# Fewer scheduling turns between k-tiles in two mixers of a three-block kernel

## The chip, the cores and the metric

The kernel runs on one core of a Trainium2 chip. The metric is the device time of one execution in microseconds (us); the kernel before took 1020.08 us, the median of three runs (1019.89 to 1020.59).

## The reference

Input is x, 256 positions by 1024, with a memory of 256 by 1024. Two blocks of a first model follow each other, then one block of a second. Every block is x = x + mixer(norm(x)) @ w_out and then x = x + ffn(norm(x)), all in float32, and norm is a root mean square norm with gains. Cut to what matters:

```
u = norm(x) @ w_in                      # 1024 x 2560 in blocks 0 and 1
block 0: o = silu(g) * norm(retention(q, k, v))           # 6 heads, chunk-causal
block 1: o = norm(softmax(q1 k1) - lam * softmax(q2 k2)) v  # 6 heads, causal by chunks
both:    o_mem = softmax(qc . mk) mv    # 4 heads over the normed memory
         x = x + concat(o, o_mem) @ w_out
         x = x + (silu(h @ w_gate) * (h @ w_up)) @ w_down  # inner width 2816
block 2: z, xbc, dt, q, k, v, f = split(norm(x) @ w_in_2)  # 1024 x 5664
         y1 = gated norm of a chunked state-space scan (16 heads) of conv(xbc), dt, z
         y2 = forgetting attention (16 heads) of q, k, v, with decays from f
         x = x + concat(y1, y2) @ w_out_2
         x = x + (silu(gate) * val) @ w_down_2             # gate, val after a causal conv
```

## The kernel before, in words

All of x stays on the chip as two tiles of 128 positions. A product with a weight runs as three matmuls in the fast fp32r type: operand and weight are each split into a high and a low part (names wh and wl for weights, lth and ltl for the normed, transposed activations), and high x high, high x low and low x high are summed in PSUM (mm3). A weight arrives by DMA in units of two k-tiles (UK = 2) by 512 columns into st; ScalarE casts it to wh, VectorE subtracts for wl. There are four st buffers and six of wh and of wl.

A projection (proj) makes 512 columns for both position tiles t: for each unit of two k-tiles and each t it issues two k-tiles of three matmuls, eight k-tiles per t, and behind the last k-tile of a t the evacuation from PSUM to SBUF.

Everything else is written as tasks: Python generators that issue some instructions (transposes, small matmuls, softmax steps, norms, splits) and then yield. A planner (class Weave) keeps a model clock per engine and runs at build time; the order in which it issues is the order of each engine's queue on the chip. A projection gives tasks a turn by W.poll(): it steps every task whose inputs are ready by the model more than 0.1 us ago (LAG), and ends with a call of W.fill(). fill issues the weight DMAs, casts and subtractions for which buffers are free. join runs tasks until a named one is done, and lets the model's TensorE stand still until then. A projection calls W.poll() behind each k-tile but the last of a t, and once behind each evacuation. The output projections (acc) call it behind each k-tile of six matmuls.

mixer0 runs seven projections: chunks 0, 1, 2, the memory's keys and values for block 0 (kv0), chunk 4, those for block 1 (kv1), chunk 3. Chunk 0 is run with a function `first` that issues the start of the program by hand. Beside them run the tasks of retention for three pairs of heads (qk, pair_task), of the memory's norm and keys, and of the memory attention (mem_attn). w_out then joins, per pair of k-tiles in the order 4, 6, 0, 2, the task that makes these: pair 2, the memory attention, pair 0, pair 1.

mixer2 runs twelve projections: two of 272 columns (bc_proj), then q, k, v, xbc and z for the first half of the heads, then the same five for the second. Beside them run gates, decays, fox (the attention), xs_part and ssd. Its w_out joins the first half's tasks and the second's in turns.

All engine calls go through one helper, so that the profile has the one line L89 for them; groups are told apart by the names of tiles: psm and psa are PSUM tiles, pcol is the identity for transposes.

Of the kernel before, what the change touches and what calls it, by code (L numbers as in the profile page):

```python
# [21 lines left out]
UK = 2  # L22
# [77 lines left out]
class Weave:  # L100
# [65 lines left out]
    def go(self, gen, at=None):  # L166
        t = Task(gen, self.now if at is None else at)
        self.tasks.append(t)
        return t
# [38 lines left out]
    def join(self, *ts):  # L208
        while not all(t.done for t in ts):
            t, at = self._next()  # L210
            assert t is not None and at < NEVER, "tasks wait for each other"
            self.clock["T"] = max(self.now, at)
            self._step(t, at)
            self.fill()
        return [t.val for t in ts]


def build(tc, a, out, stop=None):
    with tc.manual_schedule():
        _build(tc, a, out, stop)  # L220


def _build(tc, a, out, stop):
    nc = tc.nc
    W = Weave()
# [107 lines left out]
    def bcast(r, d):  # L333

        return r.unsqueeze(2).to_broadcast([r.shape[0], r.shape[1], d])

    def rep(ap, n):

        return ap.unsqueeze(1).to_broadcast([ap.shape[0], n, ap.shape[1]])
# [4 lines left out]
    def g128(ap):  # L344
        return ap.rearrange("p (g d) -> p g d", d=P)
# [15 lines left out]
    def unit_hi(parts=None, last=True):  # L361
        u, n = ready[prog["hi"]], plan[prog["hi"]][3]
        if u[1] is None:
            u[1] = whi.get(True)
        for k in parts or (slice(0, UK),):
            S.copy(u[1][:, k, :n], u[0][:, k, :n])
        prog["hi"] += last

    def unit_lo(parts=None, last=True):
        u, n = ready[prog["lo"]], plan[prog["lo"]][3]  # L370
        if u[2] is None:
            u[2] = wlo.get(True)
        for k in parts or (slice(0, UK),):
            V.tensor_tensor(u[2][:, k, :n], u[0][:, k, :n], u[1][:, k, :n].bitcast(F32), op=ALU.subtract)
        if last:
            stage.close(u[0])
        prog["lo"] += last

    AHEAD = 100

    def fill():

        while True:
            now, did = W.now, False
            if prog["dma"] < len(plan) and stage.free_at() < NEVER:
                unit_dma()
                did = True
            i = prog["lo"]
            if i < prog["hi"] and W.done[ready[i][1][:].tensor.name] <= now + AHEAD and wlo.free_at() <= now + AHEAD:
                if i <= prog["use"] + 1 or W.clock["V"] <= now + AHEAD:  # L390
                    unit_lo()
                    did = True
            i = prog["hi"]
            if i < prog["dma"] and W.done[ready[i][0][:].tensor.name] <= now + AHEAD and whi.free_at() <= now + AHEAD:
                if i <= prog["use"] + 1 or W.clock["S"] <= now + AHEAD:
                    unit_hi()
                    did = True
            if not did:
                return
# [3 lines left out]
    def unit(w, k0, c0, n, more=None):  # L403

        i = prog["use"]
        assert plan[i] == (w, k0, c0, n, more), (i, plan[i][1:], (k0, c0, n, more))
        while prog["lo"] <= i:
            if prog["dma"] <= i:
                unit_dma()
            if prog["hi"] <= i:  # L410
                unit_hi()
            else:
                unit_lo()
        prog["use"] += 1
        return ready.pop(i)[1:]

    def drop(u):
        whi.close(u[0])
        wlo.close(u[1])

    def mm3(ps, l, wh, wl, start, stop, late=False):
        T.matmul(ps, l[0], wh, start=start, stop=False)
        a, b = (l[0], wl), (l[1], wh)
        for i, (x, y) in enumerate((b, a) if late else (a, b)):
            T.matmul(ps, x, y, start=False, stop=stop and i == 1)

    def proj(w, H, c0, n, evac, serial=False, more=None, first=None):


        ps, units = [None, None], {}  # L430

        def run(t, k0):
            if first:
                first(t, k0)
            if k0 not in units:
                units[k0] = unit(w, k0, c0, n, more)
            hi, lo = units[k0]
            if ps[t] is None:
                ps[t] = psm.get(True)
            for k in range(UK):  # L440
                if first and k:
                    first(t, k0 + k)
                mm3(ps[t][:, :n], H[t].lhs(k0 + k), hi[:, k, :n], lo[:, k, :n], k0 + k == 0, k0 + k == NKT - 1, first and k0 + k)
                if k0 + k < NKT - 1 and (not first or k0 + k > 5):
                    W.poll()
            if t == 1:
                drop(units[k0])
            if k0 == NKT - UK:
                evac(t, ps[t], H[t].scale())
                psm.close(ps[t])  # L450
                W.poll()

        ks = range(0, NKT, UK)
        for t, k0 in [(t, k0) for t in range(2) for k0 in ks] if serial else [(t, k0) for k0 in ks for t in range(2)]:
            run(t, k0)

        return go(iter(()), max(W.clock["S"], W.clock["V"]))
# [549 lines left out]
    def mixer0(H, nxt, first):  # L1007
# [6 lines left out]
        sqm[0] = ring(mx, 256, "sqm", 2)  # L1014

        def chunk(c, ev, first=None):
            for t in range(2):
                u[c, t] = mx.tile([P, 512], F32, tag=f"u{c % 3 if c < 4 else c}{t}", name=W.name("u"))
            E[c] = proj(w, H, c * 512, 512, ev, first=first)
# [96 lines left out]
        for nr in mT:  # L1116
            nr.drop()
        need = {0: [pt[0]], 2: [pt[1]], 4: [pt[2]], 6: [ma]}
        join(kv1)
        return w_out(a["w_out"][0], OUT0, oT, need, H, scope, nxt), kv1  # L1120

# [183 lines left out]
    def mixer2(H, nxt):  # L1305
# [88 lines left out]
        def fox_v(f):  # L1394
            vv = [vvr.get(True) for _ in range(2)]
            return vv, proj(w, H, 4624 + 512 * f, 512, lambda t, ps, r: S.activation(vv[t][:], ps[:], AF.Copy, scale=r))
# [104 lines left out]
        def bc_proj():  # L1501

            us = uxr.get(True)

            def ev(t, ps, r):
                S.activation(us[:, t * 512 + 272 : (t + 1) * 512], ps[:, :240], AF.Copy, scale=r)
                V.scalar_tensor_tensor(two(X[:])[:, t], ps[:, 240:272], r, prow[:, R_DT : R_DT + 32],
                                       op0=ALU.mult, op1=ALU.add)

            proj(w, H, 2048, 272,  # L1510
                 lambda t, ps, r: S.activation(us[:, t * 512 : t * 512 + 272], ps[:, :272], AF.Copy, scale=r), True)
            return us, proj(w, H, 2320, 272, ev, more=(5648, 16))
# [39 lines left out]
        def decays(g):  # L1552

            yield [gt]
            res = []
            for c in range(2):
                for hq in range(2):
                    h0 = 8 * g + 4 * hq
                    tas = []
                    for part in (Rh, Rl):  # L1560
                        yield tar, 1
                        tas.append(tar.get(True))
                        V.tensor_tensor(g128(tas[-1][:]), rep(tri[:], 4),
                                        bcast(part[:, 32 * c + h0 : 32 * c + h0 + 4].bitcast(F32), P), op=ALU.mult)
                    yield psa, 1
                    ps = psa.get(True)
                    for i, ta in enumerate(tas):
                        T.matmul(ps[:], onesr[:], ta[:], start=i == 0, stop=i == 1)
                        tar.close(ta)
                    yield dcr, 1  # L1570
                    dc = dcr.get(True)
                    for e in range(4):
                        V.tensor_scalar(dc[:, e * P : (e + 1) * P], ps[:, e * P : (e + 1) * P],
                                        cs[:, 32 * c + h0 + e : 32 * c + h0 + e + 1], 0.0, op0=ALU.subtract, op1=ALU.min)
                    psa.close(ps)
                    yield
                    S.activation(dc[:], dc[:], AF.Exp)
                    res.append(dc)
            yield
            return res  # L1580
# [99 lines left out]
        def z_proj(g):  # L1680
            zs = [zsr.get(True) for _ in range(2)]
            return zs, proj(w, H, g * 512, 512, lambda t, ps, r: S.activation(zs[t][:], ps[:], AF.Silu, scale=r))

        ubc = bc_proj()
        gt = go(gates(ubc[1]))
        q, nq = fox_qk(0, 0)
        k, nk = fox_qk(0, 1)
# [7 lines left out]
        k, nk = fox_qk(1, 1)  # L1695
        vv, got = fox_v(1)
        f1 = go(fox(1, (q, k), [nq, nk], vv, got, PACE2))
        dcs = go(decays(1))
        xs = go(xs_part(1, *xbc_proj(1)))
        s1 = go(ssd(1, dcs, xs, *z_proj(1)))  # L1700
# [188 lines left out]
```

## Time and profile before

| | before |
|---|---|
| median of 3 runs | 1020.08 us |
| profiled execution | 1019.89 us |
| its span, first to last instruction | 1018.1 us |
| TensorE matmuls busy | 1008.9 us, 99% of the span |
| VectorE busy | 691.0 us, 68% |
| ScalarE busy | 611.6 us, 60% |
| GpSimd busy | 67.8 us, 7% |
| moved by DMA | 191.69 MB, mean 188 GB/s |

The span is what the trace covers; the time of an execution is a little longer. Matmuls are pipelined and their ends are modelled, so that the durations of neighbours overlap: the distance between two starts tells what an instruction costs TensorE, not its duration. A non-transpose matmul in plain float32 shows as two instructions.

### The profile page before, as it was taken

What the parts mean: (1) busy time and instruction counts of PE and PEld (TensorE: products, weight loads), DVE (VectorE), ACT (ScalarE), POOL (GpSimd) and SP (SyncE); (2) the same over time, 40 slices, a digit from 0 to 9 for tenths busy, and PEclk for the clock granted to TensorE, in tenths of its full rate; (3) what the DMA queues carried; (4) which work ended last, traced back from release to release, by engine and by line L of the source; (5) the groups of instructions that cost most, each with busy time, mean ns of one, the idle gap of its engine ahead of it and who ended that gap; (6) DMA issues with size and microseconds to landing.
All of it is one profiled execution on the core that took longest, in us unless ns stands there. A gap on an engine that the chain in (4) does not pass through costs nothing.

```text
span 1018.1 us, 13938 instructions
## 1 busy us (share of the span) xinstructions
PE 1008.9 (99%) x5049; PEld 842.0 (83%) x5049; DVE 691.0 (68%) x1045; ACT 611.6 (60%) x982; POOL 67.8 (7%) x93
## 2 busy tenths in 40 slices
PE   8999999999999999999999999999999999999998
PEld 6888888888898778888888988888888888788887
DVE  5676566555556877756565467978788567878765
ACT  7557464444455887644444446686777557757753
POOL 1121000000001231100000001100300010000000
PEclk9999999999999999999999999999999999999999
DMA  7763567776564434577667457615621658887733
GB/s 248 260 221 125 165 189 225 243 229 190 185 220 160 145 121 128 170 246 248 185 227 236 153 149 216 202 42 165 186 84 66 203 161 281 261 273 223 258 125 114
DMA packets 120581, 191.69 MB, mean 188 GB/s; under 512 B 8256, under 2 KB 39744, under 8 KB 120384
## 3 DMA queue, kind: packets, MB, share of 16 engines
q1 hardware_dynamic: 120512, 190.80, 59.0%
q8 instruction: 40, 0.66, 0.3%
q14 instruction: 29, 0.24, 0.1%
HBM read 181.34 MB, written 9.44 MB: 187 GB/s over the span
## 4 chain that ended last, share of the span: by engine, by line
PE 93%; DVE 2%; ACT 2%; POOL 1%; DMA 1%; issue 1%; SPq 0%; ACTq 0%
PE psm L89 61%; PE psa L89 32%; POOL s8r L89 1%; DVE wl L89 0%; ACT pd L89 0%; DMA st<-w_in 0%; DMA fl<-scr 0%; DVE ltl L89 0%; ACT wh L89 0%; POOL s16r L89 0%; DVE s L89 0%; ACT lth L89 0%; DVE pd L89 0%; ACT qkT L89 0%; POOL s4r L89 0%
## 5 line engine op out<-in xcount | busy, mean ns | idle before, releaser
L89 DVE TENSOR_TENSOR wl<-st,wh 128x1024 fp32r<-128x1024 f32 (+2 forms) x339 | 388.0, 1168 | 189.6 <-ACT wh L89 185.9
L89 ACT CAST wh<-st 128x1024 fp32r<-128x1024 f32 (+2 forms) x339 | 334.1, 1007 | 217.8 <-PE psm L89 86.3
L89 PE MATMUL psm<-wh,lth 128*128 128x512 f32 (+2 forms) x1024 | 394.0, 385 | 1.0 <-ACT lth L89 1.0
L89 PE MATMUL psm<-wl,lth 128*128 128x512 f32 (+2 forms) x1024 | 385.6, 377 | 0.2 <-DVE wl L89 0.2
L89 PE MATMUL psm<-wh,ltl 128*128 128x512 f32 (+2 forms) x1024 | 381.0, 377 | 0.3 <-DVE ltl L89 0.2
L89 PEld LDWEIGHTS psm<-wh,ltl 128*128 128x128 f32 x1024 | 192.6, 188 | 36.6 <-DVE ltl L89 0.8
L89 PEld LDWEIGHTS psm<-wh,lth 128*128 128x128 f32 x1024 | 192.8, 188 | 34.8 <-ACT lth L89 1.4
L89 PEld LDWEIGHTS psm<-wl,lth 128*128 128x128 f32 x1024 | 192.9, 188 | 33.8 <-DVE wl L89 1.4
L89 PE MATMUL psa<-wh,lth 128*128 128x512 f32 x328 | 130.4, 398 | 0.0
L89 PE MATMUL psa<-wl,lth 128*128 128x512 f32 x328 | 128.0, 390 | 0.7 <-DVE wl L89 0.7
L89 PE MATMUL psa<-wh,ltl 128*128 128x512 f32 x328 | 105.1, 390 | 0.0
L89 PEld LDWEIGHTS psa<-wh,ltl 128*128 128x128 f32 x328 | 61.6, 188 | 13.1
L89 PEld LDWEIGHTS psa<-wl,lth 128*128 128x128 f32 x328 | 61.7, 188 | 12.9 <-DVE wl L89 1.1
L89 PEld LDWEIGHTS psa<-wh,lth 128*128 128x128 f32 x328 | 61.6, 188 | 11.8
L89 POOL TENSOR_SCALAR s1n<-s1n 128x1 f32<-128x1 f32 x14 | 5.4, 384 | 462.6 <-ACT sq L89 462.5
L89 DVE SCALAR_TENSOR_TENSOR cc<-na,ccol,cc 128x255 f32<-128x255 f32 (+1 forms) x64 | 27.2, 480 | 6.1 <-ACT cc L89 6.0
L89 DVE SCALAR_TENSOR_TENSOR sg<-psm,s1n,sg 128x512 f32<-128x512 f32 (+1 forms) x24 | 17.0, 706 | 19.8 <-PE psm L89 19.6
L89 ACT ACTIVATE sq<-xt 128x512 f32<-128x512 f32 x24 | 15.3, 636 | 22.9 <-DVE xt L89 22.2
L89 ACT ACTIVATE sg<-psm,s1n 128x512 f32<-128x512 f32 (+1 forms) x24 | 15.7, 653 | 18.7 <-PE psm L89 18.7
L89 ACT ACTIVATE uu<-psm,s1n 128x512 f32<-128x512 f32 (+1 forms) x24 | 15.6, 651 | 15.7 <-PE psm L89 15.6
L89 ACT ACT_TABLE_LOAD x16 | 20.5, 1283 | 5.0 <-PE psm L89 2.8
L89 POOL TENSOR_TENSOR s16r<-s16r,mhalf 128x16 f32<-128x16 f32 x7 | 22.2, 3178 | 0.6
(217 smaller groups left out, 856.4 us busy)
## 6 DMA issues: line engine op xcount, KB each, us to landing
st<-w_gate_up SPq DMA_DIRECT2D x80, 512.0 KB, 4.6
st<-w_in SPq DMA_DIRECT2D x67, 512.0 KB, 4.3
st<-w_down SPq DMA_DIRECT2D x66, 512.0 KB, 5.2
st<-w_up SPq DMA_DIRECT2D x40, 512.0 KB, 4.7
st<-w_out SPq DMA_DIRECT2D x32, 512.0 KB, 3.7
scr<-sq SPq DMA_DIRECT2D x64, 128.0 KB, 4.5
fl<-scr SPq DMA_DIRECT2D x16, 512.0 KB, 5.1
st<-w_in SPq DMA_DIRECT2D x30, 256.0 KB, 4.0
```

The lines of the kernel that those rows point to most:

```text
L89: f(*args, **kw)
```

## The change

A flag rare is set at every chunk of mixer0 and taken back behind the last one, and set in mixer2 ahead of bc_proj and taken back behind the second v projection. While it is set, proj calls W.poll() only behind the second k-tile of a unit and W.fill() behind the first. Chunk 0 keeps its turns, as do the turns behind evacuations, the output projections, mixer1, the feed-forward blocks and the last two projections of mixer2.

```diff
     AHEAD = 100
+    rare = [False]
...
                 if k0 + k < NKT - 1 and (not first or k0 + k > 5):
-                    W.poll()
+                    W.poll() if k == UK - 1 or first or not rare[0] else W.fill()
...
         def chunk(c, ev, first=None):
+            rare[0] = True
             for t in range(2):
...
         need = {0: [pt[0]], 2: [pt[1]], 4: [pt[2]], 6: [ma]}
+        rare[0] = False
         join(kv1)
...
+        rare[0] = True
         ubc = bc_proj()
...
         f1 = go(fox(1, (q, k), [nq, nk], vv, got, PACE2))
+        rare[0] = False
         dcs = go(decays(1))
```

## Rows read from the trace of the kernel before

**Rows 1.** The page: TensorE's busy time, and shares of the last chain by engine.

```profile
PE 1008.9 (99%) x5049; PEld 842.0 (83%) x5049; DVE 691.0 (68%) x1045; ACT 611.6 (60%) x982; POOL 67.8 (7%) x93
...
PE 93%; DVE 2%; ACT 2%; POOL 1%; DMA 1%; issue 1%; SPq 0%; ACTq 0%
```

**Rows 2.** Windows: stretch, length, busy (count) per engine, TensorE's clock, DMA share, GB/s.

```profile
20.80:107.50 86.70, 86.18 (x462) 71.25 (x462) 56.69 (x79) 57.48 (x96) 14.39 (x18) 1.00 0.61 201
...
618.00:736.00 118.00, 118.00 (x624) 99.64 (x623) 99.94 (x201) 87.41 (x157) 15.61 (x18) 1.00 0.52 157
...
40.29:43.29 3.00, 3.00 (x29) 3.00 (x28) 1.36 (x3) 1.44 (x4) 0.17 (x1) 1.00 1.06 388
```

**Rows 3.** Waits of TensorE, the longest: total us, times, longest us.

```profile
PE psa L89 <- DVE ones L89: 1.3, 1, 1.3
```

**Rows 4.** Timeline of TensorE, plain projection: start us, us, instruction, count.

```profile
64.19 0.39 PE L89 MATMUL psm<-wh,lth 128*128 128x512 f32 x1
...
68.72 0.39 PE L89 MATMUL psm<-wh,ltl 128*128 128x512 f32 x1
```

**Rows 5.** Timeline of TensorE: a run of four transposes, one of eight.

```profile
83.78 0.60 PE L89 MATMUL psa<-pcol,u 128*128 128x128 f32 x4
...
84.45 0.40 PE L89 MATMUL psm<-wl,lth 128*128 128x512 f32 x1
...
22.20 1.03 PE L89 MATMUL psa<-pcol,u 128*128 128x128 f32 x8
...
23.31 0.39 PE L89 MATMUL psm<-wl,lth 128*128 128x512 f32 x1
```

**Rows 6.** Timeline of TensorE: a run of eight 64-row matmuls, one of sixteen.

```profile
37.24 0.92 PE L89 MATMUL psa<-qkT 64*128 64x256 f32 x8
...
38.43 0.40 PE L89 MATMUL psm<-wl,lth 128*128 128x512 f32 x1
...
49.60 1.58 PE L89 MATMUL psa<-qkT 64*128 64x256 f32 x16
...
51.45 0.39 PE L89 MATMUL psm<-wl,lth 128*128 128x512 f32 x1
```

**Rows 7.** Timeline of TensorE: three projection matmuls between two runs.

```profile
55.23 0.48 PE L89 MATMUL psm<-wh,lth 128*128 128x512 f32 x1
...
56.01 1.50 PE L89 MATMUL psa<-u,sT 128*128 128x128 f32 x12
```

**Rows 8.** Timeline of TensorE and VectorE: the memory attention and its first use.

```profile
86.36 1.13 PE L89 MATMUL psa<-kT,mqT 64*128 64x256 f32 x8
...
88.32 1.13 PE L89 MATMUL psa<-kT,mqT 64*128 64x256 f32 x8
...
104.99 0.60 PE L89 MATMUL psa<-pcol,mo 128*128 128x128 f32 x4
...
107.52 0.69 DVE L89 TENSOR_TENSOR ltl<-psa,lth 128x512 fp32r<-128x512 f32 x1 [1.52 <-ACT lth L89]
...
113.84 0.39 PE L89 MATMUL psm<-wh,lth 128*128 128x512 f32 x1
```

**Rows 9.** Timeline of TensorE: the wait for the memory's keys.

```profile
70.08 0.39 PE L89 MATMUL psm<-wh,ltl 128*128 128x512 f32 x1
70.89 0.94 PE L89 MATMUL psa<-pcol,mk 128*128 128x128 f32 x4 [0.42 <-DVE mk L89]
```

**Rows 10.** Timeline of ScalarE: two weight casts with task work between them.

```profile
85.11 1.05 ACT L89 CAST wh<-st 128x1024 fp32r<-128x1024 f32 x1
...
94.31 1.09 ACT L89 CAST wh<-st 128x1024 fp32r<-128x1024 f32 x1
```

**Rows 11.** Timeline of TensorE: end of the first half's tasks, start of the output projection.

```profile
721.47 0.60 PE L89 MATMUL psa<-pcol,xd 128*128 128x128 f32 x4
...
780.08 0.48 PE L89 MATMUL psm<-wh,lth 128*128 128x512 f32 x1
```

## The prediction

> **What bounds the kernel now.** I read the page first: TensorE is busy 99% of the span, and the chain that ended last runs 93% on it, nearly all in the matmuls into psm and psa [rows 1]. The table by stretches then shows the two stretches that the change touches. [...] So TensorE's instruction order is the time. The change removes no matmul, no transpose, no copy and no transfer. It can gain only what lies between instructions on TensorE: what a change from projection to task work and back costs, and the few waits. It can lose only where a task that comes later is waited for.
>
> **What a turn is worth: the changes of work on TensorE.** Sixteen projections are touched (six in mixer 0 after the first, ten in the last mixer). Each has 16 turns now, 14 between k-tiles and 2 behind the evacuations, and 8 after, 6 and 2: 256 turns become 128. A k-tile is three matmuls. In a plain stretch 20 matmul starts take 68.72 - 64.19 = 4.53 us, 0.2265 us each [rows 4], so a k-tile is 0.68 us. The price of a change is read from starts: the time from the first task instruction to the second matmul after the run, less one matmul. Four transposes take 84.45 - 83.78 - 0.2265 = 0.4435 us and eight take 23.31 - 22.20 - 0.2265 = 0.8835 [rows 5]. The second four cost 0.440, so a run of transposes has a fixed part of 0.0035 us: leaving the projection for it is all but free. Runs on 64 rows differ: eight qkT matmuls take 38.43 - 37.24 - 0.2265 = 0.9635 us, sixteen take 51.45 - 49.60 - 0.2265 = 1.6235 [rows 6], so eight more cost 0.66 and the fixed part is 0.30 us.
>
> How many runs merge? In TensorE's timeline I count 18 runs of task work in the first stretch and 28 in the second. With a turn at every second k-tile, two runs can no longer be only three matmuls apart, and that is the case 13 times, 3 in mixer 0 and 10 in the last mixer; [rows 7] show the first. Each of those pairs merges or moves apart. I let all 13 merge. In one of the 13 both runs are 64-row work, the two blocks of the memory attention at 86.36 and 88.32 [rows 8]; I price it at 0.30 and the other twelve, nearest to transposes, at 0.0035: 0.30 + 0.04 = 0.34 us gained. The bounds are 0 (none merges, all move apart) and 13 x 0.30 = 3.9 us (every run costs what a 64-row run costs). I stay near the low end because 42 of the 46 runs are on 66 or 128 rows.
>
> **The wait that stands in the first stretch.** TensorE waits for the keys of the memory: 70.89 - 70.08 - 0.2265 = 0.58 us [rows 9]. Later turns can remove it, if the transposes move one k-tile on, or leave it, if they stand at a turn that stays. A chain of VectorE and GpSimd work sets it, not the turn, so I leave it in: 0, with bounds of -0.58 and +0.68 (the transposes go out at the same turn and the chain starts one k-tile later).
>
> **Weight splits.** The loading and splitting of weights keeps its call at every k-tile; what changes is that task work reaches ScalarE and VectorE in larger lots, ahead of a split in the same queue. The trace has such a lot: ScalarE casts a weight at 85.11 and the next at 94.31 [rows 10], 8.15 us without one, filled with the exponentials, and TensorE went on. The six weight buffers hold 6 x 12 matmuls, 16.3 us of projection. A lot that grows by one k-tile's work is still hidden: 0. Without the cover a split that comes late costs its own length, about 1 us. No DMA moves: the SyncE queue gets the same loads at the same calls, and the changed stretches issue nothing else. GpSimd's short chains (the norms' powers) start with their tasks and are waited for only by these.
>
> **Where tasks are waited for.** In the last mixer the work of the first half ends with the transposes at 721.47, and the output projection that needs it starts at 780.08 [rows 11]: 58 us of room, and the second half's attention mostly runs where each k-tile still has its turn. Cost 0. In mixer 0 the room is small. The memory attention's last transposes start at 104.99, ScalarE and VectorE split them by 107.52 + 0.69 = 108.21, and the output projection's second pair of k-tiles needs them from 113.84 on [rows 8]: 5.63 us. From the transposes of its queries at 83.78 [rows 5] to 104.99 its chain makes eight steps from one TensorE turn to the next. If each loses one k-tile the chain is 8 x 0.68 = 5.4 us later: covered, with 0.2 us left. I take 0, because steps that already lie two or four k-tiles apart need not lose any; a loss at all sixteen turns of the chain (each step has a copy or an exponential with a turn of its own) is 10.9 us, 5.3 us past the cover, and that is the other bound. Behind the late transposes nothing else on TensorE could go ahead: the wait stands in its queue, and everything after it shifts by the same amount.
>
> **Sum.** The profiled execution took 1019.89 us, 1.79 around its span of 1018.1. Less 0.34 this is 1019.55. The median of the three runs shown is 0.19 above that execution, so the forecast for the median is 1019.7 us.
>
> **Rivals.** (a) The memory attention comes late, on the slower side. For it speaks that its room is within 0.2 us of what eight lost turns use, and that a later turn also lets a weight cast of 1.05 us into ScalarE's queue ahead of the chain's next copy; against it, that half of the steps need lose nothing, and that the output projection gives turns of the full number again. Late by 1 to 2 us (ten or eleven lost turns) the time is 1020.7 to 1021.7; from twelve on (12 x 0.68 = 8.2 us, 2.5 past the cover) it is 1022.2 and counts as slower; at sixteen, 1025.0. (b) A change of work costs more than transposes show, as with the 64-row runs: at 0.15 for each of 13 and with the 0.58 us wait gone the gain is 2.5 us, 1017.6. For it speaks [rows 6], against it [rows 5]. (c) The change thins turns that hardly bind: tasks are ready later than the turn anyway, the runs stay as many, 1020.1. [...]
>
> [...]
>
> **How the numbers follow.** About 0.2% (2.0 us) is what a measurement of this kernel can tell from no change, so the borders are 1018.0 and 1022.1. Chances: the forecast, 1018.9 to 1020.4, 0.60; (a) late by up to 2 us, 0.17; (a) from twelve lost turns on, 0.10; (b) 0.09; (c) 0.03; (d) 0.01. Faster is (b), 0.09; slower is (a) from twelve and (d), 0.11; the rest, 0.80, is within. The range of 1018.2 to 1021.8 leaves out (b), (d) and the far part of (a).
>
> **What would show it.** Right: in the first stretch fewer runs of task work, none three matmuls apart, longer ones with the same time per instruction; TensorE's idle time in both stretches unchanged to half a microsecond; the memory attention's last transposes some 3 to 5 us later and still split before the output projection's second pair. (a) would show as an idle of TensorE right there, with VectorE or ScalarE as releaser. (b) would show as a busy TensorE in both stretches with a shorter time for the same instructions. Wrong altogether would be a time that changes in the stretches that are not touched, the feed-forward blocks or the second mixer.

## The result, and the profile after

The changed kernel takes 1028.83 us, median of five runs (1027.19 to 1029.76); the kernel before took 1019.89 us in five runs beside it. The ratio is 1.0087, with a 95% interval of 1.0076 to 1.0097: slower by 8.9 us. The forecast was 1019.7 us with a range up to 1021.8; the time lies outside it, on the side that had a chance of 0.11.

The profiled execution is the fastest of the five: 1027.19 us, span 1025.4. On its page TensorE is 2.7 us busier than before for the same 5049 matmuls, and the chain that ended last no longer lies on it for 93% [rows 1]: the rest went to VectorE, ScalarE and GpSimd.

```profile
PE 1011.6 (99%) x5049; PEld 842.2 (82%) x5049; DVE 690.3 (67%) x1045; ACT 611.2 (60%) x982; POOL 77.5 (8%) x93
...
PE 85%; DVE 4%; ACT 4%; POOL 3%; DMA 1%; issue 1%; SPq 0%; DVEq 0%; ACTq 0%
```

A part of the loss stands as busy time: the two matmuls on ta at the first of the places shown below were busy for 0.71 us before and for 1.10 after. So I take the span in stages by starts: each stage runs from the last transposes of x ahead of it to those ahead of the next one (us, each from the timeline of that kernel's profile).

| | before | changed | difference |
|---|---|---|---|
| mixer 0 | 121.93 | 125.97 | +4.04 |
| feed-forward 0, mixer 1, feed-forward 1 | 472.59 | 472.57 | 0 |
| last mixer | 225.50 | 228.54 | +3.04 |
| last feed-forward | 186.75 | 186.72 | 0 |

The two mixers that were changed have 7.1 us of the 7.3 by which the span grew; the rest lies ahead of the first stage. The windows show the idle time there (length, then busy time and count per engine). In the first stretch TensorE idles 1.67 us where it idled 0.52 [rows 2], in the output projection behind it 1.99 us of 30.10 where there was none (the first line below is the kernel before), and in the last mixer 0.78 us where there was none [rows 2].

```profile
107.50:133.30 25.80, 25.80 (x128) 21.46 (x126) 16.89 (x25) 14.46 (x23) 1.62 (x4) 1.00 0.43 129
```

```profile
20.80:107.50 86.70, 85.03 (x433) 68.83 (x433) 57.09 (x80) 56.51 (x91) 17.71 (x18) 1.00 0.63 206
107.50:137.60 30.10, 28.11 (x155) 23.61 (x155) 16.71 (x24) 16.67 (x31) 1.86 (x4) 1.00 0.31 94
...
622.00:741.00 119.00, 118.22 (x623) 99.17 (x622) 96.56 (x196) 86.19 (x155) 22.93 (x18) 1.00 0.48 147
```

Two rows at the top of TensorE's list of waits are new beside the one for the ones [rows 3], the decays (ta) and the memory attention's output (mo):

```profile
PE psa L89 <- DVE ta L89: 1.4, 2, 1.0
...
PE psa L89 <- DVE mo L89: 1.2, 1, 1.2
```

**Mixer 0.** TensorE's timeline of the changed kernel (start, length, instruction, count, idle before):

```profile
86.16 0.95 PE L89 MATMUL psa<-pcol,u 128*128 128x128 f32 x4 [0.28 <-DVE u L89]
...
92.50 1.13 PE L89 MATMUL psa<-kT,mqT 64*128 64x256 f32 x8
...
95.15 1.14 PE L89 MATMUL psa<-kT,mqT 64*128 64x256 f32 x8
...
116.95 0.44 PE L89 MATMUL psa<-pcol,mo 128*128 128x128 f32 x2 [1.21 <-DVE mo L89]
118.06 0.50 PE L89 MATMUL psm<-wh,lth 128*128 128x512 f32 x1 [0.68 <-ACT lth L89]
```

The memory attention's queries are transposed at 86.16, its first scores come at 92.50, and its last transposes at 116.95, where they were at 83.78, 86.36 and 104.99 [rows 5, 8]. The output projection's second pair of k-tiles, which was at 113.84, waits for them and starts at 118.06. Of the 12.0 us by which the chain comes late, 2.4 are there at its first transposes, 3.8 come from there to the first scores, and 5.8 behind these. The middle part shows how 2.58 us became 6.34. ScalarE's timeline, before and after:

```profile
84.41 0.69 ACT L89 ACTIVATE mqT<-psa,pcol 128x512 f32<-128x512 f32 x1 [1.43 <-PE psa L89]
...
86.47 0.47 ACT L89 ACTIVATE mk<-psm,s1n 128x256 f32<-128x256 f32 x1 [0.30 <-PE psm L89]
```

```profile
88.53 0.48 ACT L89 ACTIVATE mk<-psm,s1n 128x256 f32<-128x256 f32 x1 [1.77 <-PE psm L89]
...
89.26 0.69 ACT L89 ACTIVATE mqT<-psa,pcol 128x512 f32<-128x512 f32 x1
```

The copy mqT, which the scores need, was ready to go when the transposes ended at 87.1. Its next turn came only with the projection's end, behind the evacuation mk, and in ScalarE's queue the copy stood behind mk while mk waited 1.77 us for the projection. Before, the copy went out at 84.41, ahead of the same evacuation. So the copy starts 3.10 us behind the transposes where it started 0.63 behind them; the other 1.3 us is a later turn for the scores.

The other two parts are not taken apart step by step, but the trace shows a piece of each. Ahead of the first transposes, the power in the queries' norm took 2.66 us on GpSimd, beside a weight split of VectorE that had begun just before it, where it took 1.64 in the kernel before (first line); TensorE then waits 0.28 us for the normed queries:

```profile
80.82 1.64 POOL L89 TENSOR_TENSOR s8r<-s8r,mhalf 128x8 f32<-128x8 f32 x1
```

```profile
82.92 1.22 DVE L89 TENSOR_TENSOR wl<-st,wh 128x1024 fp32r<-128x1024 f32 x1 [0.32 <-ACT wh L89]
82.99 2.66 POOL L89 TENSOR_TENSOR s8r<-s8r,mhalf 128x8 f32<-128x8 f32 x1
```

At the end of the chain, the product mo stood in VectorE's queue behind a weight split, though the matmuls that it reads ended by about 115.5; TensorE's 1.21 us wait for it is mostly this split:

```profile
115.33 1.23 DVE L89 TENSOR_TENSOR wl<-st,wh 128x1024 fp32r<-128x1024 f32 x1 [0.20 <-ACT wh L89]
116.48 0.42 DVE L89 TENSOR_TENSOR mo<-psa,s 128x256 f32<-128x256 f32 x1
```

**The last mixer.** Three places lose 3.1 us. The small matmuls on dR start 0.34 us late and take 0.11 longer. The other two are matmuls on ta. Before, one such place ran from 653.19 to 654.09:

```profile
653.19 0.60 PE L89 MATMUL psa<-pcol,aug 128*66 128x128 f32 x4
653.54 0.71 PE L89 MATMUL psa<-ta,ones 128*128 128x512 f32 x2
654.09 0.40 PE L89 MATMUL psm<-wh,lth 128*128 128x512 f32 x1
```

After, the two take 2.02 and 2.49 us from the transposes to the projection, 1.12 and 1.54 more than before (the second went from 736.20 to 737.15):

```profile
659.33 0.60 PE L89 MATMUL psa<-pcol,aug 128*66 128x128 f32 x4
660.41 1.10 PE L89 MATMUL psa<-ta,ones 128*128 128x512 f32 x2 [0.48 <-DVE ta L89]
661.35 0.40 PE L89 MATMUL psm<-wh,lth 128*128 128x512 f32 x1
...
742.55 0.60 PE L89 MATMUL psa<-pcol,aug 128*66 128x128 f32 x4
744.10 1.11 PE L89 MATMUL psa<-ta,ones 128*128 128x512 f32 x2 [0.95 <-DVE ta L89]
745.04 0.40 PE L89 MATMUL psm<-wh,lth 128*128 128x512 f32 x1
```

What made ta late is on GpSimd. The first step of a norm's rsqrt, a multiply-add on 16 columns, took this long before (with VectorE's instructions beside it) and after:

```profile
643.47 1.12 DVE L89 TENSOR_SCALAR dc<-psa,cs 128x128 f32<-128x128 f32 x4
643.64 0.21 POOL L89 TENSOR_SCALAR s16r<-s16g 128x16 f32<-128x16 f32 x1 [9.67 <-DVE s16g L89]
```

```profile
649.67 3.45 POOL L89 TENSOR_SCALAR s16r<-s16g 128x16 f32<-128x16 f32 x1 [9.70 <-DVE s16g L89]
```

VectorE's timeline of the changed kernel beside it:

```profile
649.50 0.68 DVE L89 TENSOR_TENSOR ta<-tri,dZ 128x512 fp32r<-128x512 f32 x1
650.10 1.22 DVE L89 TENSOR_TENSOR wl<-st,wh 128x1024 fp32r<-128x1024 f32 x1
651.23 0.69 DVE L89 TENSOR_TENSOR ta<-tri,dS 128x512 fp32r<-128x512 f32 x1
651.83 1.22 DVE L89 TENSOR_TENSOR wl<-st,wh 128x1024 fp32r<-128x1024 f32 x1
656.14 1.29 DVE L89 TENSOR_TENSOR aug<-aug,s16r 128x512 f32<-128x512 f32 x2 [3.09 <-POOL s16r L89]
...
660.27 0.69 DVE L89 TENSOR_TENSOR ta<-tri,dS 128x512 fp32r<-128x512 f32 x1
```

GpSimd's step ends at 653.12, when four back-to-back two-input instructions of VectorE end at 653.05. Then the power follows on GpSimd, 2.91 us as before, and VectorE has to wait for it: the norm's product (aug), at the head of VectorE's queue, holds it idle for 3.09 us, and the decays stand behind the product; the second ta comes at 660.27 and TensorE, whose queue has the ones matmul next, stands too, 0.48 us idle. The planner counts this step at 0.15 us. The second place has such a step too, 2.24 us beside two weight splits, and the product behind it waits 2.05:

```profile
733.33 2.24 POOL L89 TENSOR_SCALAR s16r<-s16g 128x16 f32<-128x16 f32 x1 [3.69 <-DVE s16g L89]
```

### The profile page after: what moved, and what is told of

Same layout as the page of the kernel before. It is cut to its first block, busy times and chain, and to the rows that moved or that the text cites. A ratio compares the mean times of both kernels' runs of the same rounds, so it can differ in the third digit from the quotient of the medians.

```text
span 1025.4 us, 13956 instructions
## 1 busy us (share of the span) xinstructions
PE 1011.6 (99%) x5049; PEld 842.2 (82%) x5049; DVE 690.3 (67%) x1045; ACT 611.2 (60%) x982; POOL 77.5 (8%) x93
## 4 chain that ended last, share of the span: by engine, by line
PE 85%; DVE 4%; ACT 4%; POOL 3%; DMA 1%; issue 1%; SPq 0%; DVEq 0%; ACTq 0%
PE psm L89 55%; PE psa L89 31%; DVE wl L89 1%; POOL s8r L89 1%; POOL s16r L89 1%; ACT wh L89 1%; DMA xt<-x 1%; DMA st<-w_in 0%; ACT pd L89 0%; DMA fl<-scr 0%; DVE s L89 0%; DVE s16g L89 0%; DVE aug L89 0%; ACT u L89 0%; POOL s2r L89 0%
```

## The experiments

Theory W: the 9 us are these late tasks and nothing else. Rival T: each lost turn costs something, so that the loss goes with their number. Ratios are to the kernel before, run on the same chip.

**1 to 4: one mixer at a time, turns back where the attention runs, the attention used later.**

```diff
 # e1: the last mixer as before
-        rare[0] = True
         ubc = bc_proj()
 # e2: mixer 0 as before
         def chunk(c, ev, first=None):
-            rare[0] = True
 # e3, on e1
-            rare[0] = True
+            rare[0] = c < 3 or c == 4
...
+        rare[0] = False
         kv1 = mem_kv(1, mx, mT)
 # e4, on e1
-    ORDER0, OUT0 = (0, 1, 2, "kv0", 4, "kv1", 3), (4, 6, 0, 2)
+    ORDER0, OUT0 = (0, 1, 2, "kv0", 4, "kv1", 3), (4, 0, 2, 6)
```

> The thinned turns stay in mixer 0 alone; the last mixer has its turn at every k-tile again. Theory W (the loss is two groups of waits for tasks that come late: the memory attention at the output projection of mixer 0, 4.3 us in the changed kernel's trace, and the decays in the last mixer, 3.0 us): 1024.2 us, or up to 1026 if the lower granted clock of the timed runs follows the wait in mixer 0; the last mixer as long as before. Rival T (each lost turn costs, spread over both mixers): 48 of 128 lost turns, 9.0 x 48/128 = 3.4 us, 1023.3.

> The thinned turns stay in the last mixer alone. Theory W: 1019.9 + 3.0 = 1022.9 us, granted clock as before if the dip belongs to mixer 0. Rival T: 80 of 128 lost turns, 5.6 us, 1025.5.

> Thinned in mixer 0 alone, and there only for chunks 1 and 2, the first memory projection and chunk 4: the second memory projection and chunk 3, beside which the memory attention runs, have every turn again. Theory W: nothing is late, 1019.6 to 1020.1 us. Rival T: 32 of 128 lost turns, 2.3 us, 1022.1.

> Thinned in mixer 0 alone, as in the first of these runs, but the output projection of mixer 0 takes its rows in the order 4, 0, 2, 6 and not 4, 6, 0, 2, so that the memory attention is needed about 5.4 us later. Theory W: the wait at the output projection goes, and of the 4.3 us about 1 us of short waits ahead of it stays: 1020.5 to 1021.5 us. Rival T: the turns are as few as in the first run, so the time is the first run's, 1023.3 to 1026.

| | time, us | ratio | mixer 0 | last mixer |
|---|---|---|---|---|
| e1 | 1025.90 | 1.0054 (1.0042 to 1.0067) | 127.68 | 225.51 |
| e2 | 1022.70 | 1.0025 (1.0016 to 1.0035) | 122.00 | 228.57 |
| e3 | 1020.33 | 1.0005 (0.9997 to 1.0014) | 121.64 | 225.56 |
| e4 | 1021.77 | 1.0020 (1.0011 to 1.0029) | 123.44 | 225.54 |

e1 and e2 came as theory W had them; e3 and e4 came 0.2 and 0.3 us above its ranges and well below rival T's. By their ratios the two halves lose 5.5 and 2.6 us of 8.9, by their stages 5.75 and 3.07; rival T had it the other way round, 3.4 and 5.6. e3 keeps two thirds of mixer 0's lost turns and loses nothing that can be told. e4 keeps all of them and needs the attention later; the wait at the output projection goes, and 1.5 us of waits ahead of it stay. Rival T falls with e3, whose interval ends at 1.4 us where T had 2.3.

e1's profile also shows what would make the changed kernel's other runs slower than its profiled one. Its windows around the wait, with the granted clock as the third number from the end:

```profile
112.80:118.70 5.90, 3.91 (x29) 3.10 (x27) 3.70 (x6) 3.06 (x4) 0.00 (x0) 1.00 0.48 153
118.75:122.15 3.40, 3.40 (x10) 2.66 (x9) 0.01 (x1) 0.00 (x0) 0.00 (x0) 0.50 0.34 119
122.20:125.60 3.40, 3.40 (x17) 2.77 (x16) 0.00 (x0) 0.32 (x1) 0.00 (x0) 1.00 0.02 5
```

TensorE had been idle for 1.99 of the 5.90 us ahead of it when the clock went to 0.50 for 3.4 us; matmuls start about 0.43 us apart instead of 0.227. That is 1.7 us, the difference of mixer 0 between e1 and the changed kernel's profile (127.68 and 125.97), where the clock stayed at 1.00. The mean clock was 0.999 in that execution and 0.997 to 0.998 in the other four: 1025.4 + 1.7 + 1.8 around the span is 1028.9, the median. e1's own runs fit this: the one with a mean clock of 1.000 took 1024.17 us, the four at 0.997 to 0.998 took 1025.68 to 1026.44. That the clock of the changed kernel's four runs fell at this place is not shown, since they have no trace. The profiles of e2 and e4, without the wait, kept 1.000.

**5 to 8: is it GpSimd's step in the last mixer, and is there a gain to be had?** Theory G: the step held up on GpSimd is the cause there. Rival M: the planner issues with too little margin after a longer gap between turns, whatever GpSimd does.

```diff
 # e5 on e2, e6 on the kernel before, e8 on e1
-        G.tensor_scalar(v, ss, inv, EPS, op0=ALU.mult, op1=ALU.add)
+        V.tensor_scalar(v, ss, inv, EPS, op0=ALU.mult, op1=ALU.add)
 # e7: the last mixer alone, and there only here
+        rare[0] = True
         xs = go(xs_part(0, *xbc_proj(0)))
         s0 = go(ssd(0, dcs, xs, *z_proj(0)))
+        rare[0] = False
```

> Thinned in the last mixer alone, and the first step of the norms' rsqrt (a multiply-add on 8 or 16 columns) moved from GpSimd to VectorE in all mixers; the power stays on GpSimd. Theory G (the last mixer's 2.9 us come from that step: 0.2 us alone, up to 3.45 us on GpSimd while VectorE subtracts weights back to back, then VectorE's queue stands at the norm's product and the decays behind it reach TensorE late): at most 1 us of the loss is left, 1019.8 to 1020.8 us. Rival M (tasks are issued with too little margin after a longer gap between turns, whatever GpSimd does): 1022.3 to 1023 us as without the move.

> Control: the kernel before with the same move of the norms' first step to VectorE, every turn kept. Both theories: near the kernel before, 1019.3 to 1020.3 us; theory G up to 0.5 us faster than it, since the wait for the memory's keys (0.58 us) is behind such a step too.

> Thinned in the last mixer alone and there only beside the first xbc and z projections, where the attention runs; gates, first decays and the norms of all four q and k projections have every turn. What thinning alone can gain on TensorE is to be seen here, since no wait for a norm or a decay falls into it. Both theories of the loss: 1019.4 to 1020.0 us, a gain of at most 0.4 us from merged runs. A rival by which each lost turn costs: 16 of 128 turns, 1.1 us slower, 1021.

> Thinned in mixer 0 alone, with the norms' first step on VectorE. If the memory attention is late because its steps lose turns (and fall behind evacuations in ScalarE's queue), most of the 5.5 us loss is left: 1024 to 1026 us. If GpSimd's held step is its cause too: 1021 us or less.

e5 took 1024.54 us (1.0049, 1.0036 to 1.0062), e6 1023.66 (1.0040, 1.0026 to 1.0054), e8 1030.26 (1.0101, 1.0088 to 1.0115). All three missed: the control e6 alone lost 4 us. The step moved in every mixer shifts the planner's order, and new waits came up in mixers 0 and 1; the mean clock of the profiled execution was 0.998 in e5 and in e6 and 0.995 in e8, where the kernel before had 1.000. The longest wait in e6:

```profile
PE psa L89 <- DVE on L89: 2.1, 1, 2.1
```

So the whole times of e5 and e8 decide nothing, and how large GpSimd's part in mixer 0's lateness is, beyond the slower power shown above, stays open. The last mixer alone reads well in them: 226.12 us in e5 against 225.47 in e6, where thinning alone had 228.57. e7 took 1020.60 (1.0006, 0.9997 to 1.0015), 0.6 us above its range: thinned beside the attention, where most short runs lie, there is no gain to be seen; its last mixer took 225.88. Its interval reaches to 1.5 us and so does not rule out a price of 1.1 us for its 16 turns; e11 below does that.

**9 to 11: the same in the last mixer alone, and both causes taken away.**

```diff
 # e9 on e2, e10 on the kernel before, e11 on the changed kernel with e3's edits
-        G.tensor_scalar(v, ss, inv, EPS, op0=ALU.mult, op1=ALU.add)
+        (V if late[0] else G).tensor_scalar(v, ss, inv, EPS, op0=ALU.mult, op1=ALU.add)
...
     def mixer2(H, nxt):
+        late[0] = True
```

> Thinned in the last mixer alone, and the first step of the rsqrt on VectorE in the last mixer alone, so that mixers 0 and 1 stay as in the kernel before (moved everywhere, the step also shifted the planner's order there). Theory G: the last mixer takes 226.1 us where thinning alone took 228.6 and the kernel before 225.5; the whole 1020.4 us (1019.9 to 1021.0). Rival M (too little margin at a turn, whatever GpSimd does): 1022.3 to 1023 us.

> Control: every turn kept, the step on VectorE in the last mixer alone. Both theories: 1019.5 to 1020.2 us, no difference from the kernel before, since there GpSimd's step mostly falls beside work that lets it through.

> The changed kernel with both causes taken away: turns back beside the memory attention of mixer 0 (as in the third run), the rsqrt's first step on VectorE in the last mixer. 112 of the 128 turns stay away. If the two causes are all of the loss: 1020.3 us (1019.7 to 1021.3), no lowered clock. If lost turns cost by themselves, 9.0 x 112/128 = 7.9 us stay: 1027.7.

| | time, us | ratio | mixer 0 | last mixer |
|---|---|---|---|---|
| e9 | 1020.20 | 1.0004 (0.9995 to 1.0013) | 121.92 | 225.90 |
| e10 | 1020.02 | 1.0005 (0.9996 to 1.0014) | 121.46 | 225.56 |
| e11 | 1020.46 | 1.0005 (0.9996 to 1.0014) | 121.56 | 225.91 |

All three came as expected of theory G and W. In e9 the step takes 0.16 us on VectorE, the norm's product waits 0.16 us and not the 3.10 of e2, ta follows in time, and TensorE has no wait in the last mixer:

```profile
645.21 0.16 DVE L89 TENSOR_SCALAR s16r<-s16g 128x16 f32<-128x16 f32 x1
...
649.29 1.29 DVE L89 TENSOR_TENSOR aug<-aug,s16r 128x512 f32<-128x512 f32 x2 [0.16 <-POOL s16r L89]
...
653.42 0.68 DVE L89 TENSOR_TENSOR ta<-tri,dS 128x512 fp32r<-128x512 f32 x1
```

e9 gives back 2.7 of the 3.0 us. The 0.4 us left to the kernel before is the place on dR, whose matmuls still start 0.27 us late and take 0.10 longer; its cause was not tested. The planner also orders VectorE's queue a little differently in e9 (the norm's sum ends 2 us earlier than in e2, and the step then stands behind other work until 645.21), but in e2 the step began at 645.24 and took until 648.69, where the shortest of its kind in that profile took 0.20 us; this length is what e9 took away.

e11 has 112 of the 128 turns gone and the time of the kernel before: rival T is out by 7 us. No version beat the kernel before beyond its interval.

## Why the prediction was wrong, point by point

- *Changes of work on TensorE: 0.34 us gained.* Fewer runs came, 14 and 25 instead of 18 and 28, and none is three matmuls from the next in the thinned stretches; in mixer 0 part of that is only that the last runs of the memory attention now lie behind the stretch. A gain of 0.34 us is neither shown nor ruled out: by the intervals of e3, e7 and e11 it is at most 0.4 us, so the upper bound of 3.9 was far off.
- *The wait for the memory's keys stays: 0.* It stayed, 0.59 us. Held.
- *Where tasks are waited for, mixer 0: cost 0.* This step failed; it cost 4.0 us, and 1.7 more where the clock fell behind it. I charged one k-tile, 0.68 us, to each of eight steps; the chain came 12.0 us later (116.95 and 104.99), beyond my bound of 10.9. A lost turn did not only cost a k-tile; it could let the step fall behind an evacuation in ScalarE's queue, which waits for the rest of the projection, or behind a weight split in VectorE's: from the queries' transposes to the first scores alone 3.8 us were lost. The cover was mis-sized too, the other way: in the kernel before 3.22 us lay between the last transposes and the end of their split (104.99 to 108.21), since its cast stood behind an evacuation in ScalarE's queue, and in the changed kernel the second pair starts 1.11 us behind the last transposes (116.95 to 118.06). That is a part of why 12.0 us of lateness became only 4.2 at the second pair (113.84 to 118.06). It was rival (a) by place, engine and sign, with 0.10 for its slower part, too little for a cover that my own sum had at 0.2 us; and its price by k-tiles ended at 1025.0.
- *The last mixer: cost 0, 58 us of room.* Failed; it cost 3.0 us. I looked for who waits only at the output projection. The wait is in the middle, in a queue: the projection matmuls that follow the ones matmuls came 1.12 and 1.54 us later behind the transposes than before. A small matmul that no one needs for a long time still stopped everything behind it.
- *"GpSimd's short chains start with their tasks and are waited for only by these."* Failed, and it is behind 2.7 of the last mixer's 3.0 us (e9). I had row 2's GpSimd busy time, but not the spread of that step's durations in the kernel before: 0.20 to 1.10 us on 16 columns (seven of them), and up to 2.24 on 8 columns (four), which would have asked what stretches it. In the changed kernel's trace the step began 0.17 us behind the first of four two-input instructions of VectorE and took 3.45 us, to 0.07 us behind the end of the last; the 1.10 us of the kernel before (from 728.50) began 0.17 us behind one weight split and ended 0.05 us behind it. That VectorE's work makes the step long is read from these times; why it does is not shown.
- *Weight splits: 0.* TensorE's waits for wl did not grow (0.7 us, elsewhere). But two of them were among the four instructions of VectorE beside which GpSimd's step took 3.45 us, and one of 1.23 us stood ahead of mo.
- *Clock, (d), 0.01 of the 0.11 for slower.* That a longer run of transposes makes the clock fall is shown by no run: the changed kernel's profile kept 1.00 in both stretches, with the merged runs. The fall to 0.50 for 3.4 us that e1's profile shows came behind the idle time of rival (a), 1.99 of 5.90 us.

The two mixers and the clock, 4.0 + 3.0 + 1.7, make 8.7 of the 8.9 us.

## What to carry to other kernels

When a planner hands out turns, a later turn costs not the gap but whatever gets ahead in each engine's queue meanwhile; look for an evacuation or a blocked product that the late step would stand behind (here mk, which waited 1.77 us, and aug, which waited 3.09). Look for waits at every instruction in the saturated engine's queue, not only where results are joined. Count a short GpSimd step on a chain at no less than its worst duration in the trace beside VectorE's two-input work, not at its median (on 16 columns 1.10 and 0.21 us in the kernel before, 3.45 and 0.55 in the changed one).

## What the runs showed of the hardware that was not expected

- A GpSimd multiply-add on 16 columns took 0.21 us beside VectorE's dc instructions, which read PSUM, and 3.45 us while VectorE ran four two-input instructions on SBUF without a gap (ta, wl, ta, wl from 649.50 to 653.05); it ended within 0.1 us of the last.
- In e1's profile the granted clock went to 0.50 for 3.4 us after TensorE had been idle for 1.99 of 5.90 us, the longest single wait being 1.21; in the changed kernel's profile the same waits were followed by a clock of 1.00.
